# One list scheduler for a decoder layer's beginning and attention, with attention on differences of v's rows

## The chip, the cores and the metric

The kernel runs on 1 core of one Trainium2 chip. The metric is the time of one execution of the whole program in device microseconds (us): the median of the runs, lower is better.

## The reference

One layer of a hybrid decoder, 1024 positions, 1024 channels, batch 1, float32:

```
h   = RMSNorm(x)
q,k,v, B,C,xc, g_att,g_conv = split(h @ w_in)      # q,k,v: 8 heads x 64; B,C,xc: 512; gates: 1024 each
# stick-breaking attention, strictly causal (s < t), per head:
z = q @ k^T / 8
A[t,s] = sigmoid(z[t,s]) * prod_{s<j<t} (1 - sigmoid(z[t,j]))
y_att  = (A @ v) @ w_att_branch
y_conv = (B * causal_dwconv3(C * xc)) @ w_conv_branch
m   = sigmoid(g_att) * y_att + sigmoid(g_conv) * y_conv
x   = x + RMSNorm(m @ w_out)
a,g = split(causal_dwconv3(RMSNorm(x) @ w_up))       # 2 x 2816 channels
x   = x + RMSNorm((gelu(g) * a) @ w_down)
```

## The kernel before

All large products are done in float16 with each operand split into a high and a low part, three products for one (`PASSES`). A weight tile is loaded (512 KB), squared and summed for its scale on ACT, the sum goes through a tiny matmul against ones (DVE writes its operand, PE multiplies, DVE reads the result), and the tile is split: high on ACT, low on DVE.

**The beginning** (up to about 47 us) turns x into hT (normalised, transposed, split), splits w_v, and computes v for the first four tiles of 128 positions and the first halves of head pair 0's q and k. Its order is made by a planner, the class `Plan`: every job is entered with its engine, cost, what it reads and writes and a due time; `order()` then simulates all engines, takes at each step the job that can start first (the more urgent among those ready), and writes the instructions in that order. The matmuls of the large products are entered as one fixed sequence; other PE jobs go ahead of the sequence as soon as the plan has them ready. `v_end` (L604, L609) evicts a tile of v from PSUM: high part on ACT, low part in two instructions on DVE. `turn_dma` (L529 to L533) turns tiles 3 to 7 of x with two DMA transposes each, from SP's queue.

**Attention** (about 47 to 380 us) is ordered by another mechanism, a loop written by hand. Attention is cut into 48 units: head pair j (4), query half c (2), key half kc (c down to 0), query tile t (3 down to 0). A unit with kc == c lies on the diagonal (`diag`, 32 units, widths of 128 to 512 keys), the other 16 are 512 keys wide; each handles two heads. The steps of a unit:

- `scores` (PE, L962): six matmuls into a two-bank PSUM tile z;
- `keep` (ACT, L980): e = sigmoid of the negated score, the part of the stick that is kept;
- `scan` (DVE, L992): a running product along the keys, from right to left, for each head, scaled by ONE = 2^14; L985, L988 and L996 set or carry a border column;
- `less` (DVE, L1000): e[s+1] - e[s], which is the attention weight;
- `w_high` (ACT, L1018) and `w_low` (DVE, L1023): the float16 parts w; each is turned by a DMA transpose from SP's queue (`turn`, L1012) into wt;
- `weigh` (PE, L962, after the last t of a group): o += v16 against wt, evicted by L1045 (ACT) and L1046 (DVE).

Between these steps the loop feeds PE with chunks of the other products ("fills"): the rest of v (L391), q and k (L225), the convolution branch's cc, cx, cb (L225), two gates, and four of eight tiles of ywc (L933). A small class `Side` puts their evictions and the weights' splits in at fixed points of the loop, by a credit for each engine; the tiny matmuls for weight sums (L2224) borrow the PSUM bank of a fill that is being evicted. There are 3 banks for the fills. The order within each engine is fixed by the program; each engine executes its own queue in order.

After 380 us the remaining stages (rest of the branches, merge, W_out, the ConvFFN) follow, ordered by the tile framework.

Of the kernel before, what the change touches and what calls it, by code (L numbers as in the profile page):

```python
# [16 lines left out]
F16 = mybir.dt.float16  # L17
# [27 lines left out]
class Layer:  # L45
# [172 lines left out]
    def cm_half(self, w, hT, ps, c):  # L218

        nc = self.nc  # L220
        n = 0
        last = 3 * KD - 1
        for k in range(KD):
            for wi, hi in PASSES:
                nc.tensor.matmul(ps, w[:, wi, ds(k * P, P)], hT[:, hi, k, ds(c * NH, NH)],  # L225
                                 start=n == 0, stop=n == last)
                n += 1
            yield


# [44 lines left out]
    def mixer(self, mid):  # L275
        tc, nc, a = self.tc, self.nc, self.a
        hT = self.hp.tile([P, 2, KD, T], F16, tag="hT", name="hT")
        with ExitStack() as ph1:
# [3 lines left out]
            self.sum_psum = (pm, [P, NH], "pm")  # L282
# [7 lines left out]

            q = self.q = Side(pm, self.ones, nc)
            bank, later, need_bank = q.bank, q.later, None

            stk = {}

            def qk_open(j, which):
                w, inv = self.wdone[f"{which}{j}"]
                if which == "q":
                    stk[j] = dict(iq=inv)
                stk[j][which] = self.slot([P, 2, T], F16, f"{which}{j}")  # L300
                stk[j]["w" + which], stk[j]["i" + which] = w[0], inv

            def qk_mm(j, which, c):
                ps = stk[j][which, c] = bank(f"p{which}{j}_{c}")
                return self.cm_half(stk[j]["w" + which], hT, ps, c)

            def qk_out(j, which, c):
                s, sl = stk[j], ds(c * NH, NH)
                ps = s.pop((which, c))
                x = s[which]  # L310

                def high():
                    nc.scalar.activation(x[:, 0, sl], ps, AF.Copy, scale=2.0 ** -15)

                def low():
                    s["done_" + which] = c
                    nc.vector.scalar_tensor_tensor(x[:, 1, sl], ps, 2.0 ** -15, x[:, 0, sl], ALU.mult, ALU.subtract)

                def scale():
                    cz = self.small(f"cz{j}", keep=True)  # L320
                    self.mul(cz[:, 0:1], s["iq"], s["ik"])
                    self.mul(cz[:, 1:2], cz[:, 0:1], cst[:, 0:1])
                    s["cz"] = cz[:, 1:2]
                return [Op("A", 0.6, high), Op("V", 0.7, low, f"p{which}{j}_{c}")] + \
                    ([Op("V", 0.2, scale)] if which == "k" and c == 0 else [])

            with tc.tile_pool(name="ptp", bufs=2, space=bass.MemoryType.PSUM) as ptp:
# [8 lines left out]
                xt, rt, pt = {}, {}, {}  # L336
# [4 lines left out]

                def square_x(tt):
                    rt[tt] = self.small(f"r_pre{tt}")
                    self.sumsq(xt[tt], rt[tt][:, 0:1], f"n_pre{tt}")

                def rstd_x(tt):
                    rt[tt] = self.rstd(rt[tt])

                def norm_x(tt):
                    nc.vector.scalar_tensor_tensor(xt[tt], xt[tt], rt[tt], gp if tt < 2 else gb, ALU.mult, ALU.mult)  # L350

                def turn_x(tt):
                    pt[tt] = ptp.tile([P, KD, P], F32, tag="pt", name=f"pt_pre{tt}")
                    for k in range(KD):
                        nc.tensor.transpose(pt[tt][:, k, :], xt[tt][:, ds(k * P, P)], self.ident)

                def high(tt):
                    nc.scalar.activation(hT[:, 0, :, ds(tt * P, P)], pt[tt], AF.Copy, scale=s_h)

                def low(tt):  # L360
                    nc.vector.scalar_tensor_tensor(hT[:, 1, :, ds(tt * P, P)], pt[tt], s_h,
                                                   hT[:, 0, :, ds(tt * P, P)], ALU.mult, ALU.subtract)

                def v_ops(tt, pv):
                    pj = pv.rearrange("p (j two d) -> p j two d", two=2, d=64)

                    sc = vs0[:, 0:1] if tt == 0 else 2.0 ** -15

                    def high():
                        nc.scalar.activation(v16[tt // 2][:, tt % 2, :, 0:4:3, :], pj, AF.Copy, scale=sc)  # L370

                    def low():
                        for e in range(2):
                            nc.vector.scalar_tensor_tensor(v16[tt // 2][:, tt % 2, :, 1 + e, :], pj[:, :, e, :],
                                                           sc, v16[tt // 2][:, tt % 2, :, 3 * e, :],
                                                           ALU.mult, ALU.subtract)
                        vdone.append(tt)
                    return [Op("A", 0.6, high), Op("V", 0.8, low, f"pv{tt}")]

                def v_out(tt, pv):  # L380
                    for op in v_ops(tt, pv):
                        op.f()

                vps, vdone = {}, []

                def v_mm(tt):
                    pv = vps[tt] = bank(f"pv{tt}")
                    n = 0
                    for k in range(KD):
                        for hi, wi in PASSES:  # L390
                            nc.tensor.matmul(pv, hT[:, hi, k, ds(tt * P, P)],  # L391
                                             wv[k // 2][:, wi, ds((k % 2) * NH, NH)],
                                             start=n == 0, stop=n == 3 * KD - 1)
                            n += 1
                        yield
# [18 lines left out]
                wv = []  # L414
                gs = self.small("g_pre", keep=True)
                cst = self.small("cst", keep=True)
                inv_ov = cst[:, 1:2]
                with tc.manual_schedule(engines={ET.PE, ET.DVE, ET.Activation, ET.SP, ET.Pool}):
                    pl = Plan(dict(s=12, ws=4, wh=8, pm=3, pt=2, sm=8, rb=8, sc=16))
# [16 lines left out]
                    def M(cost, fn, r, w, seq=True):  # L436
                        return pl.add("PE", cost, fn, r, w, seq=seq)

# [32 lines left out]
                    gpb = Buf("pt", lambda: ptp.tile([P, KD, P], F32, tag="pt", name="g_ps"))  # L471
# [36 lines left out]
                    def turn_halves(tt):  # L508
                        pt[tt] = [Buf("pm", lambda: pm.tile([P, KH, P], F32, tag="pm", name=f"pt_pre{tt}a")),
                                  Buf("pt", lambda: ptp.tile([P, KD, P], F32, tag="pt", name=f"pt_pre{tt}b"))]  # L510
                        for c in range(2):
                            def f(c=c):
                                for k in range(KH):
                                    pe.transpose(pt[tt][c].t[:, k, :], xt[tt][:, ds((c * KH + k) * P, P)], self.ident)
                            M(0.52, f, [(xs[tt], str(c))], [pt[tt][c]])

                    def turn_pe(tt):
                        pt[tt] = Buf("pt", lambda: ptp.tile([P, KD, P], F32, tag="pt", name=f"pt_pre{tt}"))
# [31 lines left out]
                    def total(n, smb, sm, cnt, keep=True):  # L550
                        rb, b, stt = Buf("rb", lambda: {}), NOTE(), {}
                        ps = Buf("pm", lambda: pm.tile([P, NH], F32, tag="pm", name=f"pr_{n}")) if cnt > 1 else \
                            Buf("pt", lambda: ptp.tile([P, KD, P], F32, tag="pt", name=f"pr_{n}"))

                        def pre():
                            r = stt["r"] = self.const.tile([P, 4], F32, tag=f"s0{n}", name=f"s0{n}", bufs=1)
                            stt["rb"] = self.smp.tile([P, 1], BF16, tag="rb", name=f"rb_{n}", bufs=8)
                            if cnt > 1:
                                vec.tensor_reduce(r[:, 0:1], sm()[:, 0:cnt], AX.X, ALU.add)
                                vec.tensor_copy(stt["rb"], r[:, 0:1])  # L560
                            else:
                                vec.tensor_copy(stt["rb"], sm()[:, 0:1])

                        def post():
                            b.t["s"], b.t["inv"] = self.pow2_of(stt["r"], ps.t if cnt > 1 else ps.t[:, 0, :])
                        V(0.35 if cnt > 1 else 0.15, pre, [smb], [rb]).lag = 0.3
                        M(0.1, lambda: pe.matmul(ps.t[:, 0:1] if cnt > 1 else ps.t[:, 0, 0:1], self.ones, stt["rb"], start=True, stop=True), [rb], [ps], seq=False)
# [29 lines left out]

                    def v_end(tt):
                        ops, n16, got = {}, NOTE(), {}
                        v = v16[tt // 2]  # L600
                        pj = lambda: pv[tt].t.rearrange("p (j two d) -> p j two d", two=2, d=64)
                        sc = lambda: vs0.t[:, 0:1] if tt == 0 else 2.0 ** -15
# [1851 lines left out]
```

## Time and profile before

| what | value |
|---|---|
| time, median of 3 runs | 1272.48 us (1271.88 to 1273.24) |
| time of the profiled execution | 1273.09 us |
| its span | 1271.0 us |
| PE busy | 1247.8 us (98%) |
| DVE busy | 1069.6 us (84%) |
| ACT busy | 827.9 us (65%) |
| POOL busy | 95.0 us (7%) |

The profiled execution is one run of the program; its span lies within its own time, the rest is start and end. Engines: PE multiplies (PEld loads its weights, beside it), DVE and ACT do elementwise work, POOL a little arithmetic and DMA issues, SP issues DMAs. A row of a group reads: line, engine, operation, output<-inputs, shapes, count, then busy time in us, mean duration in ns, and the idle time of the engine just before, with what ended it.

### The profile page before, as it was taken

What the parts mean: (1) busy time and instruction counts of PE and PEld (TensorE: products, weight loads), DVE (VectorE), ACT (ScalarE), POOL (GpSimd) and SP (SyncE); (2) the same over time, 40 slices, a digit from 0 to 9 for tenths busy, and PEclk for the clock granted to TensorE, in tenths of its full rate; (3) what the DMA queues carried; (4) which work ended last, traced back from release to release, by engine and by line L of the source; (5) the groups of instructions that cost most, each with busy time, mean ns of one, the idle gap of its engine ahead of it and who ended that gap; (6) DMA issues with size and microseconds to landing.
All of it is one profiled execution on the core that took longest, in us unless ns stands there. A gap on an engine that the chain in (4) does not pass through costs nothing.

```text
span 1271.0 us, 16592 instructions
## 1 busy us (share of the span) xinstructions
PE 1247.8 (98%) x6120; PEld 561.4 (44%) x6120; DVE 1069.6 (84%) x1738; ACT 827.9 (65%) x1186; POOL 95.0 (7%) x135
## 2 busy tenths in 40 slices
PE   9999999999999999999999999999999999999997
PEld 4443444444434444444444444444444444444443
DVE  7778888787869857888989999799799979979976
ACT  7555554545548947765566759868876977878424
POOL 1000000000000000001110001001200200121003
PEclk9999999999999999999999999999999999999999
DMA  8544553444332113422953313613930981494608
GB/s 270 139 95 113 107 105 95 106 97 97 75 84 83 50 50 107 175 84 71 234 163 88 116 34 149 232 50 55 234 126 18 167 231 34 79 249 150 186 1 133
DMA packets 145139, 150.33 MB, mean 118 GB/s; under 512 B 113697, under 2 KB 113825, under 8 KB 145058
## 3 DMA queue, kind: packets, MB, share of 16 engines
q1 hardware_dynamic: 131520, 101.03, 28.4%
q0 software_dynamic: 13536, 48.24, 17.2%
q8 instruction: 48, 0.79, 0.3%
q14 instruction: 33, 0.27, 0.1%
q10 hardware_dynamic: 2, 0.00, 0.0%
HBM read 84.49 MB, written 37.75 MB: 96 GB/s over the span
## 4 chain that ended last, share of the span: by engine, by line
PE 44%; DVE 2%; DMA 1%; issue 1%; ACT 1%; POOL 1%; POOLq 0%; DVEq 0%; ACTq 0%
PE pq L1819 11%; PE pd L1889 2%; PE pd L1922 1%; DMA hB<-n 1%; PE pu7b L1660 1%; PE pu10b L1660 1%; PE pu9b L1660 1%; PE pu20b L1660 1%; PE pu17b L1660 1%; PE pu15b L1660 1%; PE pu13b L1660 1%; PE pu6b L1660 1%; PE pu4b L1660 1%; PE pu2b L1660 1%; PE pu21b L1660 1%
## 5 line engine op out<-in xcount | busy, mean ns | idle before, releaser
L1660 PEld LDWEIGHTS <-wh_u 128*128 128x128 f16 x1848 | 179.2, 98 | 218.2 <-issue 1.7
L980 ACT ACTIVATE e<-z,cz 128x1024 f32<-128x1024 f32 (+3 forms) x48 | 43.2, 900 | 77.4 <-PE z L962 77.4
L2324 PEld LDWEIGHTS <-wh_g 128*128 128x128 f16 x588 | 57.0, 98 | 68.6
L1410 DVE SCALAR_TENSOR_TENSOR wh_u<-ws_u,sc_u,wh_u 128x1024 f16<-128x1024 f32 (+1 forms) x66 | 72.2, 1103 | 15.1 <-ACT wh_u L1408 14.7
L1408 ACT ACTIVATE wh_u<-ws_u,sc_u 128x1024 f16<-128x1024 f32 (+1 forms) x66 | 66.4, 1007 | 27.4 <-DVE sc_u L1393 5.4
L1461 PE MATMUL py<-wh_wo,m 128*128 128x512 f16 x384 | 83.6, 379 | 0.0
L1823 ACT ACTIVATE st<-pq,sd 128x512 f32<-128x512 f32 x112 | 73.7, 697 | 9.8 <-DVE ua L1703 5.6
L1374 POOL DMA_DIRECT2D acc<-st x56 | 43.7, 781 | 426.5 <-ACT st L1823 426.5
L1018 ACT ACTIVATE w<-e 128x1024 f16<-128x1024 f32 (+3 forms) x48 | 40.3, 840 | 53.8 <-DVE e L1000 53.7
L1023 DVE TENSOR_TENSOR w<-e,w 128x1024 f16<-128x1024 f32 (+3 forms) x48 | 45.9, 956 | 19.5 <-ACT w L1018 19.3
L63 ACT ACTIVATE jk_u<-ws_u 128x1024 bf16<-128x1024 f32 x44 | 46.3, 1052 | 20.7 <-DMA ws_u<-w_up_nt 20.4
L1461 PEld LDWEIGHTS <-m 128*128 128x128 f16 x384 | 37.4, 98 | 44.9
L1692 DVE SCALAR_TENSOR_TENSOR ua<-ca,cw_a,ua 128x1023 f32<-128x1023 f32 (+1 forms) x44 | 56.2, 1277 | 1.0 <-ACT ua L1690 0.8
L1692 DVE SCALAR_TENSOR_TENSOR ug<-cg,cw_g,ug 128x1023 f32<-128x1023 f32 (+1 forms) x44 | 56.2, 1276 | 0.1
L992 DVE TENSOR_TENSOR_SCAN e<-e,mask 128x512 f32<-128x512 f32 (+3 forms) x64 | 49.1, 809 | 4.2 <-ACT e L980 4.2
L1000 DVE TENSOR_TENSOR e<-e 128x1024 f32<-128x1024 f32 (+3 forms) x48 | 45.7, 953 | 0.3
L933 PE MATMUL pywc<-p,wh_wc 128*128 128x512 f16 x192 | 42.4, 379 | 3.1 <-DVE ywc L941 1.8
L225 PE MATMUL pcb<-hT,wh_cb 128*128 128x512 f16 x192 | 44.1, 379 | 0.0
L225 PE MATMUL pcx<-hT,wh_cx 128*128 128x512 f16 x192 | 44.0, 379 | 0.0
L225 PE MATMUL pcc<-hT,wh_cc 128*128 128x512 f16 x192 | 43.6, 379 | 0.0
L1819 PE MATMUL pq<-wq,fx 128*128 128x512 f16 x192 | 42.8, 379 | 0.0
L1819 PE MATMUL pq<-wq,fy 128*128 128x512 f16 x192 | 42.7, 379 | 0.0
(782 smaller groups left out, 2779.0 us busy)
## 6 DMA issues: line engine op xcount, KB each, us to landing
acc<-st POOLq DMA_DIRECT2D x56, 512.0 KB, 6.0
ws_u<-w_up_nt SPq DMA_DIRECT2D x44, 512.0 KB, 4.3
ds<-w_down SPq DMA_DIRECT2D x22, 512.0 KB, 8.3
ws_g<-w_in_nt SPq DMA_DIRECT2D x14, 512.0 KB, 3.6
x<-x SPq DMA_DIRECT2D x8, 512.0 KB, 8.7
ws_wo<-w_out SPq DMA_DIRECT2D x8, 512.0 KB, 5.3
xr<-x SPq DMA_DIRECT2D x8, 512.0 KB, 4.5
yacc<-acc SPq DMA_DIRECT2D x16, 256.0 KB, 11.5
```

The costliest lines, as they stand in the source:

```text
L63: self.nc.scalar.activation(self.junk(f"jk_{name}"), src, AF.Square, accum_out=acc)
L225: nc.tensor.matmul(ps, w[:, wi, ds(k * P, P)], hT[:, hi, k, ds(c * NH, NH)], start=n == 0, stop=n == last)
L992: nc.vector.tensor_tensor_scan(x, x, m[:, ::-1], ONE if u["diag"] else carry[u["t"]][:, h:h + 1], ALU.mult, ALU.max)
L1023: nc.vector.tensor_tensor(parts(u, 1)[1], src, hi, ALU.subtract)
L1408: A(C["As" if big else "Ash"], lambda: act.activation(dst.t[:, 0, dsl], src.t[:, ssl], AF.Copy, scale=sb.t["s"]), [(src, sreg), sb], [(dst ...
L1410: V(C["V" if big else "Vh"], lambda: vec.scalar_tensor_tensor(dst.t[:, 1, dsl], src.t[:, ssl], sb.t["s"], dst.t[:, 0, dsl], ALU.mult, ALU. ...
L1461: pe.matmul(b.t, m16[k].t[:, h_, ds(tt * P, P)], wo[k].t[:, w_, sl], start=k == 0 and p == 0, stop=k == 7 and p == 2)
L1660: pe.matmul(b.t, p.w[wt].t[:, wi, ds(wc * NH + k * P, P)], pr.block(i, h, k), start=first and n == 0, stop=n == 3 * KH - 1, skip_group_che ...
L1692: V(C["V"], lambda lag=lag: vec.scalar_tensor_tensor(u.t[:, lag:], c.t[:, :T - lag], sm.t[:, 2 - lag:3 - lag], u.t[:, lag:], ALU.mult, ALU ...
L1819: pe.matmul(b.t, fa[p].t[:, h, ds(fo * NH + tt * P, P)], wa[p].t[:, x, ds(wo * NH, NH)], start=first and n == 0, stop=n == 5, skip_group_c ...
L1823: A(C["Ah"], lambda tt=tt, b=b, st=st: act.activation(st.t[:, tt % 2, :], b.t, AF.Copy, scale=q.sd.t[:, 0:1]), [b, q.sd], [(st, str(tt % 2 ...
L2324: nc.tensor.matmul(ps, w[wt][:, wi, ds(wc * NH + k * P, P)], self.block(i, hi, k), start=first and n == 0, stop=n == 3 * KH - 1, skip_grou ...
```

## The change

1. The planner of the beginning now also holds attention and all its fills up to the end of that stage. The loop by hand and the classes `Side`, `Op` and `Task` go. `scores` and `weigh` are PE jobs outside the fixed sequence; the fills are the sequence, in chunks of two k; units are entered between fills, evenly. From the first fill on, due times are spaced by 1.2 times PE's own cost (`pace`).
2. `less` goes. Since sum_s (E[s+1] - E[s]) v[s] = sum_s (E[s] - ONE) (v[s-1] - v[s]), the weights w are now E - ONE, and v16 holds v[s-1] - v[s]. The subtraction of ONE is done inside the two instructions that make w's parts. The border column of e goes.
3. v's rows lie on partitions, so v[s-1] is fetched by DMA: for each of 8 tiles ACT writes v into vf[:, 0], one DMA copies rows 0 to 126 to rows 1 to 127 of vf[:, 1], one DMA of a single row brings the last row of the tile before; DVE subtracts; ACT and DVE split the difference into v16.
4. Smaller: the weights' sums take a PSUM bank of their own instead of a borrowed one; the fills of v go 4, 5, 6, 7 (before 6, 7, 4, 5); the four ywc tiles are all evicted by ACT (before three of four by DVE) and their squares are summed inside the stage; the carry between key halves is copied by ACT; the transposes of w have another block order off the diagonal.

The diff, cut to its core:

```diff
-                    pl = Plan(dict(s=12, ws=4, wh=8, pm=3, pt=2, sm=8, rb=8, sc=16))
+                    pl = Plan(dict(s=12, ws=4, wh=8, pm=3, z=2, o=1, sm=8, rb=8, sc=16, e=3, w=2, wt=1, cr=4, o16=4))
...
                     def v_end(tt):
-                        A(0.58, lambda: act.activation(v[:, tt % 2, :, 0:4:3, :], pj(), AF.Copy, scale=sc()), [pv[tt]] + extra,
-                          [(vb[tt // 2], f"h{tt}")], due=EV)
+                        f = vf[tt] = Buf("s", lambda: self.slot([P, 2, NH], F32, f"vf{tt}"))
+                        A(0.58, lambda: act.activation(f.t[:, 0], pv[tt].t, AF.Copy, scale=sc()), ..., [(f, "0")], due=EV)
+
+                        def moved(dst, src, r):
+                            pl.add("SP", 0.45, lambda: nc.sync.dma_start(dst(), src()), [r], [(f, "1")]).load = 0.7
+                        if tt:
+                            p_ = vf[tt - 1]
+                            moved(lambda: f.t[0:1, 1], lambda: p_.t[P - 1:P, 0], (p_, "0"))
+                        else:
+                            V(0.1, lambda: vec.memset(f.t[0:1, 1], 0.0), [], [(f, "1")])
+                        moved(lambda: f.t[1:P, 1], lambda: f.t[0:P - 1, 0], (f, "0"))
+                        V(0.62, lambda: vec.tensor_tensor(f.t[:, 1], f.t[:, 1], f.t[:, 0], ALU.subtract), [(f, "0")], [(f, "1")], due=EV + 6)
+                        A(0.55, lambda: act.activation(v[:, tt % 2, :, 0:4:3, :], pj(1), AF.Copy), [(f, "1")], [(b, f"h{tt}")], due=EV + 9)
...
-                    for tt, due in ((6, 0.0), (4, 3.0), (5, 4.0), (7, 5.0)):
+                    for tt, due in ((4, 0.0), (5, 3.0), (6, 4.0), (7, 5.0)):
                         norm(tt)
                         turn_dma(tt, due)
...
+                    def unit(u):
+                        M(0.15 + 0.6 * r, scores, [...q, k...], [z, turns[0]], seq=False)
+                        A(0.25 + 0.85 * r, ... AF.Sigmoid ..., [z, cz], [e, turns[1]], due=PACE[0])
+                        for h in range(2):
+                            V(0.08 + 1.13 * r, scan, [] if diag else [cr], [(e, str(h))], due=PACE[1])
+                        if diag and c:
+                            A(0.22, lambda: act.activation(cr.t..., e.t[:, :, NH - w:NH - w + 1], AF.Copy), [e], [cr], due=PACE[2])
+                        def turn(x):
+                            pl.add("SP", 1.25, lambda: nc.sync.dma_start_transpose(
+                                wt.t[:, x, :2 * w // P, ds(t * P, P)], w16.t[:, x, :2 * w]), ..., due=PACE[4]).load = 1.35 * r
+                        A(0.21 + 0.85 * r, lambda: act.activation(dst(0), src(), AF.Copy, bias=-ONE), [e], [(w16, "0"), turns[2]], due=PACE[2])
+                        turn(0)
+                        def low():
+                            if not diag:
+                                vec.scalar_tensor_tensor(f(1), e.t[:, :, NH - w:], ONE, f(0), ALU.subtract, ALU.subtract)
+                                return
+                            for h in range(2):
+                                vec.scalar_tensor_tensor(dst(1)[:, h], src()[:, h], ONE, dst(0)[:, h], ALU.subtract, ALU.subtract)
+                        V(0.08 + 1.1 * r + 0.08 * diag, low, [e, (w16, "0")], [(w16, "1")], due=PACE[3])
+                        turn(1)
+                        if t:
+                            return
+                        M(1.65 if diag else 2.5, weigh, [wt] + [...v16...], [o], seq=False)
...
+                    PACE = (4.0, 7.0, 9.0, 11.0, 12.0)
+                    START, END = 1, len(fills)
+                    pl.pace = 1.2
+                    for n, f in enumerate(fills):
+                        f()
+                        while k < nu and k < (n - START) * nu / (END - START - 1.5):
+                            unit(units[k])
+                            k += 1
...
-            def less(u):
-                w, e = u["w"], u["e"]
-                nc.vector.tensor_tensor(e[:, :, NH - w:NH], e[:, :, NH - w + 1:], e[:, :, NH - w:NH], ALU.subtract)
...
-                for k in range(nu + 1):
-                    n = (est[k] * lam - att_pe[k]) / chunk
-                    at(scores, k + 1)
-                    at(w_low, k - 1)
-                    run_to(base + 0.2 * n)
-                    at(scan, k)
-                    at(keep, k + 1)
...
-class Side:
```

More of the change, by code (lines that the diff above doesn't have):

```diff
@@ L289, in mixer @@
             v16 = [self.slot([P, 2, 4, 4, 64], F16, f"v16_{i}") for i in range(4)]
[L291 to L327, printed above, removed]
+            acts, inv_x, o16 = [None, None], [None, None], [None] * 4
+            sgn = self.small("sgn", w=32, keep=True)
+            smy = self.small("smy", w=16, keep=True)
+            smp_ = self.small("sm_p", keep=True)
+            ys, sig, last = {}, {}, [None]
+            if True:
                 gr = self.slot([P, D], F32, "g_row")
@@ L357, in high @@
[L357 to L395, printed above, removed]
@@ L911, in branch_fill, with v_fill @@
-            def branch_fill(d):
-                if d == 4:
-                    q.drain("p16")
-                if d % 2 == 0:
-                    need(f"wc{d // 2}")
-                yield from branch(0, d, pm, later)
-            def branch(bi, d, pm, later=None):
+                    def v_fill(tt):
+                        v_bank(tt)
+                        for i in range(4):
+                            v_pass(tt, (2 * i, 2 * i + 1), PASSES, first=i == 0, last=i == 3)
+                        v_end(tt)
@@ L928, in branch @@
                 for c in range(2):
-                    ps = bank(f"py{which}{d}_{c}") if later else pm.tile([P, NH], F32, tag="pm", name=f"py{which}{d}_{c}")
+                    ps = pm.tile([P, NH], F32, tag="pm", name=f"py{which}{d}_{c}")
                     n = 0
@@ L949, in branch @@
-                if later:
-                    tail.append(lambda: self.sumsq(y, smy[:, 8 * bi + d:8 * bi + d + 1], f"y{which}{d}"))
-                else:
-                    self.sumsq(y, smy[:, 8 * bi + d:8 * bi + d + 1], f"y{which}{d}")
-                ys[which, d] = y
-            units = [dict(j=j, c=c, kc=kc, t=t, diag=kc == c, w=(t + 1) * P if kc == c else NH, first=t == 3,
-                          end=t == 0, nm=f"{j}_{c}{kc}{t}")
-                     for j in range(4) for c in range(2) for kc in range(c, -1, -1) for t in range(3, -1, -1)]
@@ L1074, in mixer @@
-            total, chunk = 400, 0.65
-            att_pe = [0.65 * width(k + 1) + burst(k - 1) for k in range(nu + 1)]
-            est = [0.5 + 4.3 * width(k) for k in range(nu + 1)]
-            est[nu] = 4.5
-            att_v = [4.3 * width(k) + 0.5 for k in range(nu + 1)]
-            att_a = [1.75 * width(k) + 0.6 for k in range(nu + 1)]
-            lam = (sum(att_pe) + (total - 12) * chunk) / sum(est)
-            fill = fills()
-            def run_to(t):
-                while q.done < total and q.done < t:
-                    if next(fill, "end") == "end":
-                        q.done = total
-                        return
-                    q.done += 1
-                    pump()
@@ L2090, in add @@
         if seq:
-            j.late, self.now = self.now, self.now + cost
+            j.late, self.now = self.now, self.now + cost * self.pace
         for lst, wr in ((r, False), (w, True)):
```

747 lines of the change are left out of this document (248 added, 499 removed).

## The prediction

> **What bounds the kernel now.** I read the page's first part, then the busy time of each engine in stretches, then who PE waited for. The page:
>
> ```profile
> span 1271.0 us, 16592 instructions
> PE 1247.8 (98%) x6120; PEld 561.4 (44%) x6120; DVE 1069.6 (84%) x1738; ACT 827.9 (65%) x1186; POOL 95.0 (7%) x135
> ```
>
> PE is busy nearly throughout. A busy PE need not be a fast PE, so its pace comes from the list of instructions in time: two products of 24 matmuls follow each other at 36.91, 42.09 and 47.27 us.
>
> ```profile
> 36.91 5.34 PE L650 MATMUL pq<-hT,wh_q 128*128 128x512 f16 x24
> 42.09 5.34 PE L650 MATMUL pk<-hT,wh_k 128*128 128x512 f16 x24
> 47.27 4.05 PE L391 MATMUL pv<-wh_v,hT 128*128 128x512 f16 x18
> 53.31 2.75 PE L225 MATMUL pq<-hT,wh_q 128*128 128x512 f16 x12
> ```
>
> That is (47.27 - 36.91) / 48 = 0.216 us a matmul with nothing between them, and the change removes no matmul. So only PE's idle time can be won. The stretches (start:end length, then busy us of PE, PEld, DVE, ACT, POOL; clock, DMA share, GB/s):
>
> ```profile
> 0.00:20.00 20.00, 18.32 (x49) 8.74 (x50) 12.25 (x37) 12.67 (x21) 3.20 (x12) 1.00 0.88 345
> 20.00:47.27 27.27, 27.25 (x131) 12.56 (x130) 26.12 (x44) 23.45 (x34) 4.98 (x7) 1.00 0.79 182
> 47.27:380.00 332.73, 321.01 (x1804) 138.60 (x1803) 260.95 (x472) 168.55 (x228) 10.61 (x20) 1.00 0.44 96
> 380.00:560.00 180.00, 180.00 (x848) 81.73 (x846) 145.41 (x235) 131.40 (x199) 0.53 (x1) 1.00 0.28 94
> ```
>
> In the attention stretch PE idles 332.73 - 321.01 = 11.7 us; behind it, up to 560 us, not at all. The planner's own stretch (20 to 47.27 us) loses 0.02 us with DVE busy 26.12 of 27.27. Who PE waited for, up to 385 us (total, times, longest):
>
> ```profile
> PE o L962 <- issue: 4.0, 3, 1.7
> PE pq L2224 <- DVE sc_cx L94: 2.1, 1, 2.1
> PE pywc L933 <- DVE ywc L941: 1.8, 1, 1.8
> PE warm L467 <- DVE wz L332: 1.7, 1, 1.7
> PE pywc L933 <- DVE o L1046: 1.3, 1, 1.3
> PE pcc L2224 <- DVE sc_cb L94: 0.9, 1, 0.9
> PE pcx L2224 <- DVE u L844: 0.7, 1, 0.7
> PE pcb L2224 <- DVE pf L844: 0.7, 1, 0.7
> PE pq L2224 <- DVE q L317: 0.3, 1, 0.3
> ```
>
> Without the start-up wait (L467) these nine rows make 11.8 us: three `weigh` bursts that came before their transposes, 4.0; weight sums and banks that waited for a DVE with other work ahead, the rest.
>
> **The change, part by part.** *`less` removed, w - ONE inside the parts.* The rows:
>
> ```profile
> L1000 DVE TENSOR_TENSOR e<-e 128x1024 f32<-128x1024 f32 (+3 forms) x48 | 45.7, 953 | 0.3
> ```
> ```profile
> L1023 DVE TENSOR_TENSOR w<-e,w 128x1024 f16<-128x1024 f32 x24 | 29.3, 1222 | 10.9 <-ACT w L1018 10.9
> L785 DVE SCALAR_TENSOR_TENSOR wh_cc<-ws_cc,sc_cc,wh_cc 128x1024 f16<-128x1024 f32 x4 | 5.1, 1282 | 1.8 <-ACT wh_cc L782 1.8
> L1046 DVE SCALAR_TENSOR_TENSOR o<-o,o 128x512 f16<-128x512 f32 x8 | 5.4, 681 | 7.0 <-ACT o L1045 7.0
> L988 DVE COPY e<-cr 128x2 f32<-128x2 f32 x16 | 2.6, 161 | 0.0
> L996 DVE COPY cr<-e 128x2 f32<-128x2 f32 x16 | 2.7, 170 | 0.5
> L985 DVE MEMSET e<- 128x2 f32 x32 | 1.9, 60 | 0.0
> L370 ACT ACTIVATE v<-pv 128x512 f16<-128x512 f32 x4 | 2.4, 588 | 0.3 <-PE pv L391 0.3
> ```
>
> DVE loses 45.7 us and, with the border columns, 2.6 + 2.7 + 1.9 = 7.2. `w_low` becomes a three-operand instruction: 1.282 for 1.222, so 16 x 0.06 = 1.0 us; on the diagonal it is two halves, at most 2 x 0.681 for 1.222, so 32 x 0.14 = 4.5. The eight subtractions on v cost 8 x 0.68 = 5.5 (by L1046's size). DVE net: -42 us, from 261 to about 219 of 333. ACT gains 8 x 0.59 = 4.7 for v's second pass (L370's size), 16 carries of about DVE's 0.17, six evictions of ywc and four squares; by estimate under 20 us on 169. All of it lies beside PE: worth nothing by itself, and covered as long as PE has fills. Its worth is that whatever PE waited for in DVE's queue comes sooner, and the weigh chain is one DVE pass (1.2 us at full width) shorter.
>
> *Order by list.* The 11.7 us go if attention runs as the stretch before 47 us does. New waits come in their place: 48 scores, 12 weighs and some 25 weight sums, each put into PE's queue where the plan has it ready, with every fill queued behind it. Lower bound: the planner's stretch, 0.02 us for a handful of such places, so about 0.3 for 85. Upper: 85 waits of 0.14 us give back all 11.7. DVE has a third of its time free here and had 4% there, and between chunks of 1.3 us a placed job has on average half a chunk of slack, so I take 2.0.
>
> *The beginning.* Four tiles of v now cost DVE a subtraction each before 60 us, and SP up to eight more issues. SP's queue:
>
> ```profile
> 26.45 3.72 SPq L533 DMA_TRANSPOSE hT<-x  x2
> 30.26 0.53 SPq L620 DMA_DIRECT2D ws_q<-w_in_nt  x1
> 37.57 12.84 SPq L533 DMA_TRANSPOSE hT<-x  x8
> ```
>
> Eight transposes take SP from 37.57 to 50.4 us, and the first product that needs all of them starts at 53.31; a transpose lands 3.3 us after its issue:
>
> ```profile
> hT<-x SPq DMA_TRANSPOSE x10, 3.3
> ws_cc<-w_in_nt POOLq DMA_DIRECT2D x4, 512.0 KB, 3.9
> ```
>
> So there is no margin. What is queued behind a shift on SP is a transpose of x; behind a subtraction that waits for its shift, on DVE, x's split and the evictions. At 0.53 us an issue, the three or four that fall after 33 us cost 1.5 to 2 us on SP, of which other work (the fill of v4 needs tile 4 alone) hides some. A shift of 254 KB is not in the trace; nearest by shape are the loads of 128 rows, 512 KB, landing in 3.9. Taking that, nothing else is late and the beginning costs 1.5 us (0 to 3). The other end is the first rival.
>
> *End of the stage.* The tail's 1.8 + 1.3 us (ywc's bank, o's eviction) belong to the 11.7. Four sums of squares move ahead, at most the same ACT time; from 380 us PE has no idle time to lose or win and everything shifts. Banks: a sum takes one of three for about 1.5 us out of a fill's 5.2; free in the plan. Moved transposes, POOL's loads: same number, nothing.
>
> **Sum:** -11.7 + 2.0 + 1.5 = -8.2 us. The profiled execution took 1273.1 with a span of 1271.0; 1273.1 - 8.2 = 1264.9, and the median lies 0.6 below the profiled execution: 1264.3. Own range 1260 to 1269.
>
> **Rival 1, slower: the shifts run on one DMA engine.** 127 rows cannot be dealt evenly to 16 engines. The queues' rows (packets, MB, share):
>
> ```profile
> q0 software_dynamic: 13536, 48.24, 17.2%
> q10 hardware_dynamic: 2, 0.00, 0.0%
> ```
>
> The issues' rows, of which the first and the last with their sizes stand here, add up to 94 loads and stores of 128 rows in POOL's queue:
>
> ```profile
> acc<-st POOLq DMA_DIRECT2D x56, 512.0 KB, 6.0
> ...
> g_ffn_post<-g_ffn_post POOLq DMA_DIRECT2D x1, 512.0 KB, 4.5
> ```
>
> 13536 / 94 = 144 packets, 128 rows and 16 others. ACT's only DMA, one row, left 2. So the extra packets look like one for each engine used, and a single row used one. If 127 rows use one too, a shift takes 254 KB at one engine's rate; 345 GB/s at a share of 0.88 is 24.5 GB/s an engine, so 10.6 us, and everything later in SP's queue waits behind it. The first eviction of v and its fourth product mark the places:
>
> ```profile
> 23.54 0.67 ACT L604 ACTIVATE v<-pv,vs 128x512 f16<-128x512 f32 x1
> ```
> ```profile
> 31.73 5.34 PE L591 MATMUL pv<-wh_v,hT 128*128 128x512 f16 x24
> ```
>
> The first shift (about 24.5 us) would hold tile 3's transposes, and with them v's product at 31.7, until 37: +5. The next three end near 69 us; tile 4's low part stands behind them, so v4 starts near 70 instead of 52: +18. The last four come every 5.2 us and take 10.6; their subtractions block DVE, and after two free banks PE: about +10. Together +33 - 8 = +25: 1297, range 1280 to 1310. It decides from about 6 us a shift on. Against it: no row shows 127 rows, and 128 rows land in 3.9.
>
> [...]
>
> **Rival 2, no change: the order has no margin.** The 85 placed jobs wait 0.14 us each, new waits replace the old: 1272. For it: each waits by construction for the newest result. Against: the 0.02 us of the planner's stretch.
>
> **Chances.** The forecast 0.50, with 0.05 more for a gain beyond its range; rival 1 0.35; rival 2 0.10. A measurement tells about 0.2% (2.5 us) from no change, so faster 0.55, same 0.10, slower 0.35. Both signs are likely, so the range spans them: 1260 to 1303.
>
> **What would show it.** Right: PE idle between 47 and 370 us below 4 us, no L1000, DVE about 42 us less there, no wait above 1 us for a weigh, SP's shifts landing in under 4 us. Rival 1: shifts landing in about 10 us, PE idle before v3 near 32 us and before v4, DVE waiting for DMA at the subtraction. Rival 2: many PE waits of 0.1 to 0.3 us at scores and sums. The prediction fails if the shifts are slow, or if PE runs out of fills before attention ends.

## The result, and the profile after

| | time, median (us) | ratio to before, 95% interval |
|---|---|---|
| before | 1272.18 | |
| changed kernel | 1334.38 (1333.07 to 1336.87) | 1.049 [1.0472, 1.0508] |

The changed kernel is 62 us slower, where 8 us faster was predicted; rival 1, the shifts on one DMA engine, is what the runs below speak for, at more than twice its price. The page's first part:

```profile
span 1332.8 us, 16588 instructions
PE 1258.0 (94%) x6120; PEld 564.9 (42%) x6120; DVE 1030.2 (77%) x1661; ACT 837.0 (63%) x1215; POOL 98.3 (7%) x137
```

The span grew by 1332.8 - 1271.0 = 61.8 us. PE's idle time (span less busy) grew from 23.2 to 74.8, that is by 51.6, and PE's busy time by 1258.0 - 1247.8 = 10.2, for the same 6120 matmuls. DVE did 39.4 us less work. Where PE idles, by stretches (length, then busy us of PE, PEld, DVE, ACT, POOL; granted clock, DMA share, GB/s):

```profile
20.00:47.27 27.27, 19.98 (x90) 8.81 (x89) 16.14 (x26) 17.73 (x26) 3.52 (x3) 0.87 0.78 84
47.27:100.00 52.73, 30.18 (x143) 12.71 (x142) 19.53 (x33) 13.61 (x18) 4.86 (x6) 0.77 0.69 95
100.00:150.00 50.00, 31.70 (x168) 12.49 (x166) 23.10 (x45) 18.34 (x31) 1.05 (x2) 0.83 0.64 83
150.00:200.00 50.00, 37.53 (x209) 15.55 (x209) 34.24 (x58) 24.06 (x34) 2.11 (x4) 0.86 0.46 98
200.00:380.00 180.00, 178.33 (x1020) 77.47 (x1019) 129.82 (x228) 99.06 (x143) 7.39 (x14) 1.00 0.52 105
```

PE lost 7.3, 22.6, 18.3 and 12.5 us up to 200 us, together 60.6, and only 1.7 from there to 380. The first column behind POOL is the granted clock, a mean over the stretch with its idle time: it falls below 1.00 in just those stretches. What arrives late, first by the groups (the last entry: idle time of the engine just before, and who ended it), then by the landing times that the trace has for copies of the tile vf, then by the DMA issues:

```profile
L524 DVE TENSOR_TENSOR vf<-vf 128x512 f32<-128x512 f32 x8 | 5.5, 692 | 72.4 <-DMA vf<-vf 72.4
```
```profile
DMA to landing us min/median/max: 12.7/12.9/24.9
```
```profile
hT<-x SPq DMA_TRANSPOSE x10, 5.1
vf<-vf SPq DMA_DIRECT2D x7, 2.0 KB, 12.9
```

The eight subtractions took 0.692 us each, as predicted (0.68), but DVE stood still for 72.4 us in front of them. The landings are those of the seven single rows of 2 KB that share the queue with the shifts: none took less than 12.7 us. For the shifts themselves the trace has no landing, but the lists in time bound the first: it is one of the two issues from 23.67 us on, and the subtraction that waits for it starts at 37.58, about 13 us later. Transposes of x went from 3.3 to 5.1. SP's queue, as a list in time, shows how one stands behind the other (a block of 20.31 us for three issues):

```profile
23.67 1.39 SPq L517 DMA_DIRECT2D vf<-vf  x2
26.12 11.26 SPq L440 DMA_TRANSPOSE hT<-x  x2
...
50.57 20.31 SPq L517 DMA_DIRECT2D vf<-vf  x3
70.97 14.22 SPq L440 DMA_TRANSPOSE hT<-x  x6
```

Two transposes that held SP for 3.72 us before held it for 11.26 here. While PE stood still from 64 to 70 us, the core's 16 DMA engines were 6% busy on average, which is one of sixteen, and moved 26 GB/s. PE's list over the same time (in brackets the idle time before the row, and who ended it):

```profile
38.58 7.27 PE L499 MATMUL pv<-wh_v,hT 128*128 128x512 f16 x24 [7.03 <-DMA hT<-x]
...
56.05 2.75 PE L499 MATMUL pv<-wh_v,hT 128*128 128x512 f16 x12
73.80 0.61 PE L756 MATMUL z<-k,q 64*128 64x512 f16 x2 [15.00 <-ACT k L578]
81.97 2.00 PE L756 MATMUL z<-k,q 64*128 64x512 f16 x10 [7.55 <-DVE k L580]
...
83.94 2.72 PE L499 MATMUL pv<-wh_v,hT 128*128 128x512 f16 x6
...
87.15 1.47 PE L499 MATMUL pv<-wh_v,hT 128*128 128x512 f16 x6
```

The first stop is at v's fourth product, which was named in rival 1. The second is not the low part of tile 4: the first scores wait 15.0 and 7.55 us for the eviction of k. DVE's list says why:

```profile
37.58 0.69 DVE L524 TENSOR_TENSOR vf<-vf 128x512 f32<-128x512 f32 x1 [7.44 <-DMA vf<-vf]
...
69.53 0.69 DVE L524 TENSOR_TENSOR vf<-vf 128x512 f32<-128x512 f32 x1 [15.10 <-DMA vf<-vf]
...
73.20 0.68 DVE L580 SCALAR_TENSOR_TENSOR q<-pq,q 128x512 f16<-128x512 f32 x1
73.80 2.47 DVE L437 SCALAR_TENSOR_TENSOR x<-x,g_pre,x 128x1024 f16<-128x1024 f32 x2
79.95 0.69 DVE L524 TENSOR_TENSOR vf<-vf 128x512 f32<-128x512 f32 x1 [3.68 <-DMA vf<-vf]
...
81.23 0.69 DVE L580 SCALAR_TENSOR_TENSOR k<-pk,k 128x512 f16<-128x512 f32 x1
```

pq and pk were finished by 56 us. Their evictions stand in DVE's queue behind subtractions that wait for a shift, and ACT's stand behind the split of the difference. So a DMA of v's rows holds the scores, which read q and k and not v. From 100 us on the same happens to the weights' sums and scales, by PE's waits (total, times, longest):

```profile
PE pr_cx L475 <- DVE cv L106: 11.3, 1, 11.3
PE pr_k L475 <- DVE rb_k L470: 8.0, 1, 8.0
...
PE pr_cc L475 <- DVE rb_cc L470: 6.8, 1, 6.8
PE pq L563 <- DVE sc_cc L94: 4.6, 1, 4.6
```

The engine named is DVE each time; in DVE's list a subtraction that waited 8.9 to 10.4 us for its shift (at 102.53, 135.71, 150.34 and 166.79 us) stands a few us ahead of each.

### The profile page after: what moved, and what is told of

It is laid out like the page before. It is cut to its first block, busy times and chain, and to the rows that moved or that the text cites. A ratio compares the mean times of both kernels' runs of the same rounds, so it can differ in the third digit from the quotient of the medians.

```text
span 1332.8 us, 16588 instructions
## 1 busy us (share of the span) xinstructions
PE 1258.0 (94%) x6120; PEld 564.9 (42%) x6120; DVE 1030.2 (77%) x1661; ACT 837.0 (63%) x1215; POOL 98.3 (7%) x137
## 3 DMA queue, kind: packets, MB, share of 16 engines
q1 hardware_dynamic: 132480, 102.07, 31.2%
q0 software_dynamic: 13824, 49.29, 16.6%
## 5 line engine op out<-in xcount | busy, mean ns | idle before, releaser
L1569 ACT ACTIVATE st<-pq,sd 128x512 f32<-128x512 f32 x112 | 73.9, 697 | 10.2 <-DVE ua L1449 5.6
L524 DVE TENSOR_TENSOR vf<-vf 128x512 f32<-128x512 f32 x8 | 5.5, 692 | 72.4 <-DMA vf<-vf 72.4
L756 PE MATMUL z<-k,q 64*128 64x512 f16 (+3 forms) x288 | 33.4, 345 | 23.3 <-ACT k L578 15.0
L499 PE MATMUL pv<-wh_v,hT 128*128 128x512 f16 x168 | 44.7, 421 | 7.3 <-DMA hT<-x 7.0
L563 PE MATMUL pq<-hT,wh_q 128*128 128x512 f16 x192 | 46.2, 399 | 4.6 <-DVE sc_cc L94 4.6
L525 ACT ACTIVATE v<-vf 128x512 f16<-128x512 f32 x8 | 5.0, 628 | 68.7 <-DVE vf L524 68.7
```

The source lines that it names most:

```text
L499: pe.matmul(pv[tt].t, hT[:, hi, k, ds(tt * P, P)], wvb[k // 2].t[:, wi, ds((k % 2) * NH, NH)], start=first and n == 0, stop=last and n == ...
L563: pe.matmul(ps.t, w.t[:, wi, ds(k * P, P)], hT[:, hi, k, ds(c * NH, NH)], start=k == 0 and p == 0, stop=k == KD - 1 and p == 2)
L1569: A(C["Ah"], lambda tt=tt, b=b, st=st: act.activation(st.t[:, tt % 2, :], b.t, AF.Copy, scale=q.sd.t[:, 0:1]), [b, q.sd], [(st, str(tt % 2 ...
```

## The experiments

All times with a ratio were taken beside runs of the kernel before on the same chip; those without are one time, in which differences of some 6 us mean nothing (single runs of the kernel before ranged from 1271.6 to 1278.0).

### The two halves apart, and the shift cut in two

*The shift cut into 112 and 15 rows*, all else as changed:

```diff
-moved(lambda: f.t[1:P, 1], lambda: f.t[0:P - 1, 0], (f, "0"))
+moved(lambda: f.t[1:113, 1], lambda: f.t[0:112, 0], (f, "0"))
+moved(lambda: f.t[113:P, 1], lambda: f.t[112:P - 1, 0], (f, "0"))
```

> The changed kernel, but each shift of 127 rows is issued as two DMAs, 112 rows and 15 rows. Theory A (127 rows run on one DMA engine, and SP's queue and DVE wait behind them): the shifts land in under 5 us instead of 12.7, PE idles under 5 us between 20 and 200 us instead of about 60, and the time is 1260 to 1268 us. Theory B (moving rows inside SBUF is slow however it is cut): the shifts still land in about 12 us, 1325 to 1335 us. Theory C (the list's order without margin costs the time, the slow shift only shows it): PE still idles 20 us or more in many places, 1285 us or more.

*The list scheduler alone*: `less` and the border column are back, and v is evicted from PSUM as before.

```diff
+V(0.08 + 1.07 * r, lambda: vec.tensor_tensor(e.t[:, :, NH - w:NH], e.t[:, :, NH - w + 1:], e.t[:, :, NH - w:NH], ALU.subtract), [], [e], ...)
-act.activation(dst(0), src(), AF.Copy, bias=-ONE)
+act.activation(dst(0), src(), AF.Copy)
...
```

> The list scheduler for beginning and attention with the old attention: the difference pass on DVE stays, v is not differenced, no shifts. Theory A: PE idles 3 to 7 us between 47 and 380 us, 1264 to 1270 us; the scheduler brings most of the gain by itself. Theory C: 1272 us or more.

*The difference alone*: the kernel before with its loop by hand, `less` removed, v's difference taken with the shift in two parts, the fills of v in the order 4, 5, 6, 7.

```diff
+nc.sync.dma_start(f[1:113, 1], f[0:112, 0])
+nc.sync.dma_start(f[113:P, 1], f[112:P - 1, 0])
+nc.sync.dma_start(f[0:1, 1], vf[tt - 1][P - 1:P, 0])
...
-nc.vector.tensor_tensor(e[:, :, NH - w:NH], e[:, :, NH - w + 1:], e[:, :, NH - w:NH], ALU.subtract)
```

> The kernel before with its hand-written attention loop; only the difference pass is replaced by differences of v's rows, with the shift cut into 112 and 15 rows and the fills of v in the order 4 to 7. Theory A: DVE loses about 40 us in the attention stretch but the positions in PE's queue stay, so a third to a half of the 11.7 us of PE idle goes: 1266 to 1271 us. Theory B: over 1300 us.

| kernel | time (us) | ratio to before, 95% interval |
|---|---|---|
| before, in this group | 1273.86 | |
| shift cut in two | 1266.51 | 0.9938 [0.9926, 0.9950] |
| list scheduler alone | 1261.02 | 0.9899 [0.9886, 0.9912] |
| difference alone | 1280.73 | 1.0045 [1.0029, 1.0061] |

All three ratios are clear of 1 by their intervals, though within 2% of it. The shift cut in two came out as theory A had it, but for 5.5 us of PE's idle time between 20 and 200 us where under 5 was expected. The scheduler alone did better than its range of 1264 to 1270 us, and the difference alone missed its range (1266 to 1271) on the slow side.

One line of the change decided between 1334 and 1267 us. The issues of the kernel with the shift cut in two (KB each, median us to landing):

```profile
vf<-vf SPq DMA_DIRECT2D x8, 224.0 KB, 2.9
vf<-vf SPq DMA_DIRECT2D x8, 30.0 KB, 2.8
```

The same 254 KB land in 2.9 instead of about 13 us. One stretch, 20 to 380 us, for the kernel before, the shift cut in two, the scheduler alone and the difference alone:

```profile
20.00:380.00 360.00, 348.26 (x1934) 151.16 (x1933) 287.06 (x514) 192.00 (x262) 15.59 (x27) 1.00 0.46 103
```
```profile
20.00:380.00 360.00, 353.01 (x1969) 156.10 (x1968) 259.04 (x446) 208.82 (x303) 19.38 (x29) 1.00 0.52 110
```
```profile
20.00:380.00 360.00, 357.97 (x1994) 157.87 (x1993) 300.81 (x514) 209.96 (x303) 18.43 (x29) 1.00 0.48 105
```
```profile
20.00:380.00 360.00, 343.90 (x1891) 148.15 (x1889) 250.63 (x469) 192.60 (x266) 17.46 (x27) 0.99 0.52 109
```

PE idles 11.7, 7.0, 2.0 and 16.1 us. Seen as a table of two by two, by the medians, the list order (with the smaller changes of point 4, which this kernel keeps) is worth -12.8 us (1261.02 against 1273.86) and the difference costs, on the old order, +6.9 (1280.73; by the ratio 5.7); the two together -6.0, and -7.4 was measured. On the list order the difference costs 1266.51 - 1261.02 = 5.5. So even with quick shifts the difference of v, with the pass over e that it saves, loses time. On the old order it shows here:

```profile
PE pv L404 <- DMA hT<-x: 9.0, 2, 5.3
PE o L987 <- issue: 3.2, 2, 1.6
```

The transposes of tiles 4 to 7 of x, between which the new DMAs now stand on SP, run from 36.94 to 60.25 us (37.57 to 50.4 before); how much of this is the new issues and how much is waiting for their inputs was not separated. The weighs that come before their transposes are still there (4.0 before, 3.2 here, 0.3 with the scheduler alone): removing `less` did not cure them, the order did.

### Is it the row count, and is it the queue?

*A different row count for each tile*, the rest of the 127 rows in a second DMA:

```diff
+n = (127, 126, 125, 124, 122, 112, 120, 96)[tt]
+moved(lambda: f.t[1:n + 1, 1], lambda: f.t[0:n, 0], (f, "0"))
+if n < P - 1:
+    moved(lambda: f.t[n + 1:P, 1], lambda: f.t[n:P - 1, 0], (f, "0"))
```

> The changed kernel with the shift of each of the eight tiles cut at another row: 127; 126+1; 125+2; 124+3; 122+5; 112+15; 120+7; 96+31. Theory A, with the number of engines the largest number up to 16 that divides the rows, and about 10 us for 254 KB on one engine plus 2 us: landing 12 to 13 us for 127 (one engine), 2.5 to 3.5 for 126 (14), 4 to 5 for 125 (5), 4.5 to 5.5 for 124 (4), 7 to 8 for 122 (2), under 3.5 for 112, 120 and 96, 4 to 5 for the 31 rows. A theory by size alone puts 127 and 122 within 5% of each other.

Measured: 1281.68 us, with 17.3 us of PE's idle time in the stretch. The trace gives a landing for two of the sizes alone:

```profile
vfG<-vfG SPq DMA_DIRECT2D x1, 240.0 KB, 3.8
vfF<-vfF SPq DMA_DIRECT2D x1, 224.0 KB, 3.1
```

120 and 112 rows are quick. Of 127 rows (tile A) it shows the issue at 23.89 us and the subtraction that waits for it at 37.16:

```profile
37.16 0.69 DVE L527 TENSOR_TENSOR vfA<-vfA 128x512 f32<-128x512 f32 x1 [7.60 <-DMA vfA<-vfA]
```

So the run confirms both ends; as a curve of time against rows it failed, since the sizes between gave no landing. Its packets say more:

```profile
q1 hardware_dynamic: 132609, 102.07, 30.2%
```

That is 1377 packets more than the list scheduler alone (131232, shown below). A single row of 2 KB adds 32: in the changed kernel SP's queue has 132480, which is 8 x 128 for the shifts and 7 x 32 for the rows more than 131232. If every other piece adds its rows and, by theory A, the largest number up to 16 that divides them, this run's pieces add 952 + 73 for the eight large ones, 63 + 33 for six rests and 8 x 32 for the single rows: 1377. The count holds to the packet, as a sum over all sizes; that its second part counts engines is the prediction's reading.

*127 rows from POOL's queue* (a median of four times), and *127 rows from ACT's queue* (one time):

```diff
-moved(lambda: f.t[1:P, 1], lambda: f.t[0:P - 1, 0], (f, "0"))
+j_ = pl.add("G", 1.14, lambda: nc.gpsimd.dma_start(f.t[1:P, 1], f.t[0:P - 1, 0]), [(f, "0")], [(f, "1")])
+j_.load, j_.lag = 0.7, 4.0
```
```diff
-moved(lambda: f.t[1:P, 1], lambda: f.t[0:P - 1, 0], (f, "0"))
+pl.add("A", 0.6, lambda: nc.scalar.dma_start(f.t[1:P, 1], f.t[0:P - 1, 0]), [(f, "0")], [(f, "1")]).load = 0.7
```

> The changed kernel with the 127-row shifts issued from POOL's queue, in one piece. If the row count alone decides in every queue: landing over 10 us and DVE's waits at the subtractions stay, 1285 to 1320 us. If POOL's queue deals 127 rows over 16 engines: landing 3 to 6 us, PE idle under 10 us up to 380 us, 1262 to 1272 us.

> The changed kernel with the 127-row shifts issued from ACT's queue. Theory A: still one engine and over 10 us a shift, but x's and w's transposes in SP's queue no longer stand behind them: the transposes of x land in about 3 to 4 us and the waits for them vanish, while DVE's waits at the subtractions stay (40 us or more): 1290 to 1320 us. If standing in one queue was all of the cost: 1262 to 1272 us.

POOL: 1266.94 us, 0.9945 [0.9925, 0.9965], the same as the shift cut in two. ACT: 1342.21 us, no better than SP and above both ranges that were expected. The queues and issues of the two, POOL first:

```profile
q0 software_dynamic: 14464, 51.37, 18.4%
...
vf<-vf POOLq DMA_DIRECT2D x8, 254.0 KB, 3.0
hT<-x SPq DMA_TRANSPOSE x10, 3.3
```
```profile
q10 hardware_dynamic: 1026, 2.08, 0.4%
...
hT<-x SPq DMA_TRANSPOSE x10, 9.4
vf<-vf SPq DMA_DIRECT2D x7, 2.0 KB, 2.3
```

ACT's queue held 2 packets in all runs without the shifts; eight shifts add 1024, which is 128 each: 127 rows and one other, so one engine by the prediction's reading of the extra packets. The first shift was issued at 28.24 us and its subtraction, which waited for it, started at 43.28, some 15 us later. The transposes were expected to recover, since SP's queue was free of shifts, and the 2 KB rows did (2.3 us). The transposes did not: 9.4 us. Waiting in one instruction queue therefore isn't the whole of it. What else holds the transposes was not shown: no row here has the engines one by one, and the 2 KB rows landed in 5.0 us at most, though two of them were issued from 30.27 us on, while the first shift was under way. From POOL the same 127 rows added (14464 - 13824) / 8 = 80 packets each, not 128, and landed in 3.0. The 80 packets are not 127 + 16 either, so the reading of packets as rows and engines does not carry over to POOL's copy.

### The shift's disturbance without anybody waiting for its result

Here the list scheduler alone issues, at the places of the shifts, eight DMAs on SP that nobody reads:

```diff
+pl.add("SP", 0.45, lambda: nc.sync.dma_start(scr[1:P], self.mask[0:P - 1]), [(vb[tt // 2], f"h{tt}")], [(idle, f"{tt}")]).load = 0.7
```

> The scheduler alone (1261 us) with eight extra DMAs of 127 rows of 1280 bytes (162 KB) from a constant into a scratch tile, in SP's queue after each tile of v; nothing reads what they write. Theory A (what stands behind such a DMA on its engine waits too): x's transposes land in over 5 us instead of 3.3 and PE waits for them 10 to 25 us in all: 1270 to 1290 us. If only DVE's waits at the subtractions cost the time: 1261 to 1264 us.

The two others differ in one number each: `scr[1:113], self.mask[0:112]` and `scr[1:123], self.mask[0:122]`.

> The kernel of the run with unread shifts, with 112 rows in each unread DMA instead of 127 (12% fewer bytes, the same queue and places; nothing reads the result). Theory (the row count sets how many engines a DMA spreads over): these spread over sixteen, take about 3 us like the other loads, and the kernel comes to 1260 to 1265 us, like the scheduler alone; transposes land in 3.3 to 3.5 us. Rival (the extra bytes or the extra entries in SP's queue are what costs): close to the 1294 us of the run with 127 rows, since bytes and entries are nearly the same.

> The same with 122 rows, for which the packets of the run with several row counts gave two engines. Theory: a DMA takes about half of the time of 127 rows, some 5 to 6 us, and the time lies between the two, 1262 to 1278 us; the rival by bytes and entries: near 1294 us again.

| rows of each unread DMA | KB | time (us) | PE idle, 20 to 380 us | PE busy, whole span |
|---|---|---|---|---|
| none (1258.8 us span) | | 1261.02 | 2.0 | 1244.7 |
| 112 | 140.0 | 1269.27 | 5.1 | 1249.5 |
| 122 | 152.5 | 1268.79 | 9.2 | 1246.5 |
| 127 | 158.8 | 1293.82 | 26.9 | 1252.2 |

From 122 to 127 rows are 4% more bytes and 25 us more time, so neither bytes nor entries in SP's queue are the price of 127; the rival falls. (The first row was taken beside other runs of the kernel before, 1273.86 us there and 1272.85 beside the three others.) SP's queue, by packets, for no unread DMAs, 122 rows and 127 rows:

```profile
q1 hardware_dynamic: 131232, 99.98, 29.1%
```
```profile
q1 hardware_dynamic: 132224, 101.23, 30.3%
```
```profile
q1 hardware_dynamic: 132256, 101.28, 30.8%
```

The eight add 992 = 8 x (122 + 2) and 1024 = 8 x (127 + 1); with 112 rows the queue held 132256 too, that is 1024 = 8 x (112 + 16). By the prediction's reading of the packets these are two engines, one and sixteen. How long SP is held by two unread DMAs in a row, with 127 rows, with 122 and with 112:

```profile
33.20 10.70 SPq L523 DMA_DIRECT2D scr<-mask  x2
43.99 8.39 SPq L440 DMA_TRANSPOSE hT<-x  x1
```
```profile
29.87 6.22 SPq L523 DMA_DIRECT2D scr<-mask  x2
```
```profile
30.51 2.86 SPq L523 DMA_DIRECT2D scr<-mask  x2
```

Three misses: 127 rows cost 33 us where at most 29 (1290) was expected, though the transposes of x landed in 4.8 us and not in over 5, and 112 rows cost 8 us, above the range that ended at 1265. Those 8 us are little more than the spread of single times, and no run shows their cause. In time 122 rows do as well as 112; in SP's row and in PE's idle time they lie between 112 and 127. The 127 rows are far out of proportion: 33 us against 8.

So of the changed kernel's loss some 33 us need no reader: in the run with 127 unread rows PE waits 12.4 us for transposes of x and 10.7 for those of w. The rest, up to the 73 us between 1261 and 1334, is put down to DVE and ACT waiting for the shift in their own queues, as their lists above show; no run has that part by itself. (The unread DMAs move 159 KB and not 254, so the cut between the two is rough.)

### The planner told the true price

```diff
-moved(lambda: f.t[1:P, 1], lambda: f.t[0:P - 1, 0], (f, "0"))
+pl.add("SP", 0.45, lambda: nc.sync.dma_start(f.t[1:P, 1], f.t[0:P - 1, 0]), [(f, "0")], [(f, "1")]).lag = 13.0
```

> The changed kernel with its 127-row shifts as they are; only the planner is told that a shift lands 13 us after its issue (it had counted with about 3). Theory A: the subtractions are placed later and DVE's waits for them fall from 72 us to under 20, but the shifts still stand in SP's queue ahead of x's and w's transposes, so 20 to 40 us of PE idle stay: 1285 to 1310 us. If the wrong price alone was the cause: 1262 to 1270 us.

Measured: 1324.59 us, above both ranges. DVE's waits for its shifts:

```profile
DVE vf L524 <- DMA vf<-vf: 21.3, 4, 10.1
```

72.4 us of waiting became 21.3 (under 20 was expected), and PE's idle time in the stretch only fell from 62.3 to 50.9 (20 to 40 expected): the transposes of x now landed in 7.1 us, and PE waited 10.4 + 8.2 us for them. The new order took other work ahead of DVE's waits, but the transposes came later than before. The plan was told when a shift lands, not that SP's queue is held meanwhile (a shift is still 0.45 us of SP in it); an order that knows this too was not tested.

### What remains of the difference's cost

*The weights as E - ONE without any difference of v*, so that the pass over e is gone and nothing is paid for it (the sums of attention are then not the reference's), and *POOL's shifts with the three jobs behind them due 10 us later* (`EV + 6`, 9, 12 became 16, 19, 22):

> The changed kernel without the eight differences of v (left out: v16 holds v itself, so the attention's sums are not the reference's); the difference pass stays removed and w is E - ONE. It tells what the removed pass is worth once the list scheduler is there. If DVE's relief is worth time: 1256 to 1260 us. If PE was already fed, as in the scheduler alone: 1260 to 1263 us, no better than it.

> The changed kernel with the 127-row shifts from POOL's queue and the difference, its high and its low part due 10 us later in the plan. It asks whether the 4 to 5 us by which the repaired kernel stays behind the scheduler alone come from v's difference being too urgent in the busy beginning. If so: PE idle between 20 and 100 us falls from 3.1 to under 1.5 us and the time to 1261 to 1264 us. If not: 1265 to 1268 us as before.

The first: 1262.57 us, 0.9912 [0.9897, 0.9927], not faster than the scheduler alone (0.9899). Its row of the group `less` is gone, DVE is 41 us lighter (1025.2 against 1066.6), and the time is the same. The second: 1266.46 us, 0.9941 [0.9927, 0.9954], where 1266.94 was without the delay. PE's idle time between 20 and 100 us did not fall either (5.0 us, 3.1 without the delay). The urgency of those jobs isn't what costs; this theory fell. What PE waited for in this run up to 380 us:

```profile
PE pr_k L475 <- DVE rb_k L470: 2.7, 2, 1.9
PE pq L564 <- DMA hT<-x: 1.7, 1, 1.7
PE o L757 <- DMA wt<-w: 1.3, 2, 0.9
```

So some 5 us of the difference's price remain in small waits of the first 100 us and of attention; they have no single cause that these runs show.

## Why the prediction was wrong, point by point

- **PE as the limit, and the order by list: right, and cautious.** Of the 11.7 us the scheduler alone left 2.0. That this is the number taken for the new waits is luck: it was meant for attention, where 0.6 was measured; 1.4 lie before 47 us. It gained 12.8 us against the 9.7 of those two terms. Of the 12.2 us between the profiled spans (1271.0 and 1258.8) 9.1 are PE's idle time and 3.1 its busy time for the same 6120 matmuls; "only PE's idle time can be won" had no room for those 3.1, and no run shows their cause.
- **DVE's relief: right.** 39.4 us less over the whole span for the 42 worked out, ACT 9.1 us more for "under 20", and worth nothing by itself: the run without the difference shows it directly.
- **The step that failed: "The beginning", 1.5 us (0 to 3).** It took the loads of 128 rows as the nearest row for a shift of 127 rows. By shape they are; in time they were not: the shift took about 13 and not 3.9 us, and the beginning and what hung on it cost about 70 us. With the shift cut so that it does land in 2.9 us, the time is 1266.51, inside the forecast's own range of 1260 to 1269. Even that is in part luck: the difference then costs 5.5 us where the term had 0 to 3, and the list order gains about 3 us more than forecast. The packet counts that spoke against the term stood in the prediction, at 128 rows and at one, and nothing in the trace spoke for 127 rows being spread; they were given less than their due.
- **Rival 1: the mechanism right, the sum too small.** A shift was put at 10.6 us (about 13 measured from its issue; at the 26 GB/s of the trace 254 KB take some 10 us, so some 3 us are left for which the sum had no term). The reading that a single row uses one engine was taken from the 2 packets of ACT's row; the 2 KB rows on SP, which left 32 packets each, don't fit it. At v's fourth product +5 was worked out (7.0 measured), +18 for the next three shifts (15.0 + 7.55 at the scores; the low part of tile 4 wasn't what decided, but the eviction of k behind a subtraction), and "about 10" for the last four. Those cost 18.3 + 12.5 = 31 us: DVE kept to its queue's order (q's eviction, its product finished by 56 us, came at 73.20 behind a subtraction that had waited 15.10), and the waits went through to PE by way of weight sums and scales. The sum, +33, became 60.6 us of idle time. Its trigger, "about 6 us a shift", was not tested in this kernel.
- **Left out: the clock.** 10.2 us of PE's busy time are the same matmuls, slower. Six of them took 2.72 us behind the long waits, at a granted clock of 0.50, and 1.47 a moment later at 1.00. By the forecast this had no price, in rival 1 either.
- **The range** ended at 1303, 6 us above rival 1's sum of 1297 and below the end of rival 1's own range, 1310. Its upper end came from the same 10 us for the last shifts and from no price for the clock.

## What to carry to other kernels

Before a DMA with a row count that the trace does not have goes into a busy queue, time one of that count, and where that can't be done, take the slow end as the forecast if the packet counts speak for it: from SP, 127 rows took about 13 us here, the same rows as 112 and 15 took 2.9 and 2.8. The slow DMA was paid for by what stood behind its reader in DVE's queue, here by the scores (15.0 and 7.55 us), whose products pq and pk had been finished by 56 us, so price a wait by what stands behind it and not by who needs the data. A pass removed from an engine beside the limit was worth nothing (1262.57 against 1261.02 us); the best version of these runs is the list scheduler with the difference pass left in, 1261.02 us, 1.0% below the kernel before.

## What the runs showed of the hardware

- A DMA of 127 rows (254 KB) from SP took about 13 us from its issue to the subtraction that waited for it (23.89 to 37.16 us in the run with several row counts), from ACT some 15, and from POOL it landed in 3.0. While one from SP was in flight and PE stood still, the 16 DMA engines were 6% busy and moved 26 GB/s. The unread DMAs of 122 rows cost no more time than those of 112 (1268.79 and 1269.27 us; with 127 rows 1293.82), but two in a row held SP for 6.22 us where those held it for 2.86 (10.70 with 127).
- With the slow DMAs on ACT's queue, transposes issued from SP landed in 9.4 us instead of 3.3.
- The granted clock was lower where PE idled: 0.77 in the stretch with 22.6 us of PE's idle time, 1.00 in the one with 1.7 of 180. PE stopped at 58.8 us; the clock was still 1.00 from 60 to 62 us, 0.75 on the mean from 62 to 64 and 0.50 from 64 us on, so it fell about 4 us after the last matmul. PE's work came back at 81.97, and the clock was 0.50 up to 86.6 and 1.00 from 87 on, about 5 us after the work did. Six matmuls took 2.72 / 1.47 = 1.85 times as long at 0.50. So these waits on PE cost more than their length: 51.6 us of added idle time came with 10.2 us of added busy time.
